# Seven products instead of eight for four of sixteen row tiles of the FFN input projection

## The chip, the cores and the metric

The kernel runs on one core of a Trainium2 chip. The metric is the device time of one execution in microseconds (us), as the median of several. One more execution was profiled; the rows shown in this document come from that one.

## The reference, cut to what matters

The network is two layers over 256 tokens with 2048 channels. Each layer has a mixer (one wide input projection, three branches, an output projection) and then a gated feed-forward block (FFN). The change is in the FFN:

```python
h = rms_norm(x, g_ffn_pre)                       # (256, 2048)
a, b = jnp.split(h @ w_ffn_in, 2, axis=-1)       # w_ffn_in (2048, 11264): a and b are (256, 5632)
x = x + rms_norm((jax.nn.silu(a) * b) @ w_ffn_out, g_ffn_post)
```

All inputs are float32.

## The kernel before, in words

**Products in two pieces.** TensorE multiplies in a reduced float32 format (F32R). So each factor is kept as two pieces, hi (rounded) and lo (what rounding left), and each product is three matmuls into one accumulator: hi by hi, lo by hi, hi by lo (L670, L671, L672). The tokens are the stationary factor, 128 channels by 128 tokens; the weights move, 128 rows by 512 columns.

**Chunks, items and blocks.** The list `chunks` holds every 512-column piece of every weight matrix, in order: for the FFN the pairs (a columns j, b columns j), j from 0 to 10, cut into two parts of 6 and 5 pairs (L599), each part followed by its share of the output projection `w_ffn_out` in four column pieces, which accumulates over the parts in the tiles `og` (L557 to L563). An item is one row tile (128 rows) of one chunk; an FFN-in chunk has 16. A block is two items, loaded together by `load` (L636): one DMA of 512 KB into a `raw` tile (`fetch`, RAWBUFS of them), one cast on ScalarE (ACT) to `whi` (L646), one subtraction on VectorE (DVE) to `wlo` (L647). There are WBLOCKS = 7 buffers for `whi` and `wlo`. All weight transfers are issued from one queue, SyncE's (SP).

**Two token halves.** `multiply(h)` does one item for the 128 tokens of half h, three matmuls. The main loop (L758) lets half 0 run up to LAG = 8 items ahead of half 1 and then alternates. So a block's twelve matmuls stand in two groups of six, and its buffers come free when half 1 has used it. The first pair of each layer's FFN (a chunk that begins a stage, `paired`) takes a and b block by block in turn; the other 20 pairs of the two layers take chunk a and then chunk b.

**Evacuation.** After the 16 items of a chunk, `ev_a` (L540) makes silu(a): a Sigmoid on ACT and a multiplication on DVE; `ev_b` (L547) multiplies by b on DVE and, D_T = 7 steps later, transposes the result on TensorE (L137) and splits it into hi and lo (L130 on ACT, L131 on DVE). These tiles, `hid`, are the stationary factor of the output projection. PSUM has eight banks: two each for the accumulators of half 0 (`mm0`) and half 1 (`mm1`), two for transposes (`tp`), two for other small products (`sc`). Tiles of 4 KB per partition come from one pool of SLOTS.

The order of instructions on each engine, and which buffer of a tag a tile takes, is laid down at build time by the framework, which starts from the order in which the code emits them; only the first block of the program (L753) is kept in the written order.

Of the kernel before, what the change touches and what calls it, by code (L numbers as in the profile page):

```python
# [11 lines left out]
F32 = mybir.dt.float32  # L12
# [3 lines left out]
ALU = mybir.AluOpType  # L16
# [17 lines left out]


LOAD = 2
RAWBUFS = 4
LAG = 8
WBLOCKS = 7
SLOTS = 22  # L40


BUDGET = 0.35
# [29 lines left out]
def trunk(ctx: ExitStack, tc: tile.TileContext, x, x_cols, positions, g_mix_post, g_ffn_post, w_in, pool_w,  # L73
# [14 lines left out]
    def nm(s):  # L88
        uid[0] += 1
        return f"{s}_{uid[0]}"  # L90
# [4 lines left out]
    def t2(tag, bufs, shape=(P, NB), dtype=F32):  # L95
        return tmp.tile(list(shape), dtype, name=nm(tag), tag=tag, bufs=bufs)
# [2 lines left out]
        return sm.tile([P, n], dtype, name=nm(tag), tag=tag, bufs=bufs)  # L99

    def ps_tp():
        return psum.tile([P, 4, P], F32, name=nm("tp"), tag="tp", bufs=2)

    def ps_sc():
        return psum.tile([P, 4, P], F32, name=nm("sc"), tag="sc", bufs=2)

    ident = cpool.tile([P, P], F32, name="ident")
    make_identity(nc, ident)
# [15 lines left out]
    def split(src, gain=None):  # L124
        t = slot([P, 2, 4, P], F32R)
        if gain is not None:
            u = t2("ta", 3, (P, 4, P))
            dve.tensor_tensor(u, src, gain.unsqueeze(2).to_broadcast([P, 4, P]), op=ALU.mult)  # L128
            src = u
        act.copy(t[:, 0], src)  # L130
        dve.tensor_tensor(t[:, 1], src, t[:, 0].bitcast(F32), op=ALU.subtract)  # L131
        return t

    def transpose4(src):
        tp = ps_tp()
        for j in range(4):
            pe.transpose(tp[:, j, :], src[:, j * P:(j + 1) * P], ident)  # L137
        return tp
# [9 lines left out]
    def defer(steps, fn, *args):  # L148
        later.append((clock[0] + steps, fn, args))
# [5 lines left out]
        for _, fn, args in due:  # L155
            fn(*args)

    def pre_norm_quad(h, c, gain):
        st["xT", h].append(split(transpose4(xs[h][:, c, :]), gain[:, 4 * c:4 * c + 4]))

    def pre_norm_rstd(h, ssq):
        tot = small("ssq_t", 1)
# [27 lines left out]
            st["ms_o", h] = small("ms_o", 1)  # L190
            gp.tensor_scalar(st["ms_o", h], tot, 1.0 / D, NORM_EPS, op0=ALU.mult, op1=ALU.add)  # L191

    def post_norm(h, gain):
        r = st["rpost", h]
        ogs = [st["og", h, c] for c in range(4)]

        def residual(c):
            xc = xs[h][:, c, :]
            dve.scalar_tensor_tensor(xc, ogs[c], r, xc, op0=ALU.mult, op1=ALU.add)  # L199
            if gain is None:  # L200
                nc.sync.dma_start(out[0, h * P:(h + 1) * P, c * NB:(c + 1) * NB], xc)

        if gain is None:
            for c in range(4):
                residual(c)
            return
        st["xT", h] = []
        residual(0)
        for c in range(4):
            defer(N_FIRST + N_STEP * c, pre_norm_quad, h, c, gain)  # L210
            if c < 3:
                defer(N_FIRST + N_STEP * c, residual, c + 1)
        defer(N_FIRST + N_STEP * 4, sum_squares, h)
# [317 lines left out]
    def ev_out(l, c):  # L531
        def f(h, ps):
            bc = gain_tile(c, h, g_mix_post[l])
            og_tile(c, h)
            post_collect(h, c, ps, bc)
            if c == 3:
                post_norm(h, par[l][:, C_GFFN:C_GFFN + 16])
        return f

    def ev_a(h, ps):  # L540
        s = t2("tb", 2)
        act.activation(s, ps, ACT.Sigmoid, scale=st["rstd", h])  # L542
        t = t2("sg", 3)
        dve.scalar_tensor_tensor(t, ps, st["rstd", h], s, op0=ALU.mult, op1=ALU.mult)  # L544
        st["sg", h] = t

    def ev_b(first):  # L547
        def f(h, ps):
            if first:
                st["hid", h] = []  # L550
            t = t2("ta", 3)
            dve.scalar_tensor_tensor(t, ps, st["rstd", h], st["sg", h], op0=ALU.mult, op1=ALU.mult)  # L552
            hid = st["hid", h]
            defer(D_T, lambda: hid.append(split(transpose4(t))))
        return f

    def ev_ffn(l, c, part, last):  # L557
        def f(h, ps):
# [20 lines left out]
    for l in range(DEPTH):  # L579
        wi = w_in[l]  # L580
        add(wi, 0, 16, Q_POOL, "xT", ev_pool(l))
        for qd in range(2):
            add(wi, 0, 16, Q_V + qd * NB, "xT", ev_v(qd))
        for qd in range(2):
            add(wi, 0, 16, Q_Q + qd * NB, "xT", ev_rot("qT", qd))
        for qd in range(2):
            add(wi, 0, 16, Q_K + qd * NB, "xT", ev_rot("kT", qd))
        for qd in range(2):
            add(wi, 0, 16, Q_R + qd * NB, "xT", ev_swish(l, qd))
        add(wi, 0, 16, Q_CG, "xT", ev_conv_g)  # L590
        add(wi, 0, 16, Q_CA, "xT", ev_conv_a(l))
        for b, c in [(b, c) for c in range(4) for b in (0, 2)] + [(1, c) for c in range(4)]:
            add(wi, 0, 16, Q_GATE + b * D + c * NB, "xT", ev_gate)
            w, name = ((w_pool_proj, "pool"), (w_conv_proj, "conv"), (w_ret_proj, "ret"))[b]
            add(w[l], 0, 8 if b == 2 else 4, c * NB, ("brT", b), ev_y(b, c), (name,))
        for c in range(4):
            add(w_out[l], 0, 16, c * NB, "mT", ev_out(l, c))
        ends.append(len(chunks))
        parts = ((0, 6), (6, 11))  # L599
        for p, (b0, b1) in enumerate(parts):  # L600
            for j in range(b0, b1):
                add(w_ffn_in[l], 0, 16, j * NB, "xT", ev_a)
                add(w_ffn_in[l], 0, 16, HIDDEN + j * NB, "xT", ev_b(j == b0))
            for c in range(4):
                add(w_ffn_out[l], b0 * 4, (b1 - b0) * 4, c * NB, "hid", ev_ffn(l, c, p, p == len(parts) - 1))
        ends.append(len(chunks))

    paired = {0} | {e for e in ends[:-1]}  # L610
    items = []
    n = 0
    while n < len(chunks):
        side = (n, n + 1) if n in paired else (n,)
        for k in range(0, chunks[n][2], LOAD):
            for m in side:
                items += [(m, k + kk) for kk in range(LOAD)]
        n += len(side)
    raws = {}
    wt = {}  # L620
    banks = {}
    loaded = [0]
    done = [0, 0]

    def fetch(i):
        n, k = items[i]
        w, r0, kt, c0 = chunks[n][:4]
        r = (r0 + k) * P
        raw = wpool.tile([P, LOAD, NB], F32, name=nm("raw"), tag="raw", bufs=RAWBUFS)
        step = LOAD if i else 1  # L630
        for kk in range(0, LOAD, step):
            nc.sync.dma_start(raw[:, kk:kk + step], w[r + kk * P:r + (kk + step) * P, c0:c0 + NB]
                              .rearrange("(k p) n -> p k n", p=P))
        raws[i] = raw

    def load():  # L636

        i = loaded[0]
        if i not in raws:
            fetch(i)  # L640
        raw = raws.pop(i)
        hi = wpool.tile([P, LOAD, NB], F32R, name=nm("whi"), tag="whi", bufs=WBLOCKS)
        lo = wpool.tile([P, LOAD, NB], F32R, name=nm("wlo"), tag="wlo", bufs=WBLOCKS)
        step = LOAD if i else 1
        for kk in range(0, LOAD, step):
            act.copy(hi[:, kk:kk + step], raw[:, kk:kk + step])  # L646
            dve.tensor_tensor(lo[:, kk:kk + step], raw[:, kk:kk + step], hi[:, kk:kk + step].bitcast(F32),  # L647
                              op=ALU.subtract)
        for kk in range(LOAD):
            wt[i + kk] = (hi[:, kk, :], lo[:, kk, :])  # L650
        loaded[0] += LOAD
# [3 lines left out]
    def load_ahead():  # L655
        while loaded[0] < min(len(items), done[1] // LOAD * LOAD + ahead[0]):
            load()

    def multiply(h):
        i = done[h]  # L660
        n, k = items[i]
        w, r0, kt, c0, lhs, evac, needs = chunks[n]
        if k == 0:
            finish({(s, q) for s in needs for q in (0, h)})
            banks[h, n] = psum.tile([P, NB], F32, name=nm("mm"), tag=f"mm{h}", bufs=2)
        ps = banks[h, n]
        a = (st[lhs + (h,)] if isinstance(lhs, tuple) else st[lhs, h])[k // 4]
        hi, lo = wt[i]
        ah, al = a[:, 0, k % 4, :], a[:, 1, k % 4, :]
        pe.matmul(ps, ah, hi, start=(k == 0), stop=False)  # L670
        pe.matmul(ps, al, hi, start=False, stop=False)  # L671
        pe.matmul(ps, ah, lo, start=False, stop=(k == kt - 1))  # L672
        if k == kt - 1:
            evac(h, ps)
        if h == 1:
            del wt[i]
        done[h] += 1
        load_ahead()
        tick()


    def begin():
# [71 lines left out]
        begin()  # L754
    ahead[0] = LOAD * WBLOCKS
    defer(16, add_job, ("trig", 0), rotary_tables(), True)
    count = [sum(chunks[n][2] for n in range(e)) for e in ends]
    for end in count:  # L758
        while done[1] < end:
            if done[0] < end:  # L760
                multiply(0)
            if done[0] == end or done[0] - done[1] > LAG:
                multiply(1)
                run_jobs(BUDGET)


def _tables():
# [52 lines left out]
```

## Time and profile before

| | us |
|---|---|
| median of 3 runs (2900.63 to 2902.14) | 2900.93 |
| the profiled execution | 2900.57 |
| span of that execution, first to last instruction | 2898.8 |

A row of the profile names a line of the kernel, an engine, what is written and read, the count, the busy time and the mean length of one instruction. PE is TensorE's matmuls and transposes, PEld its weight loads, which run beside them. A matmul's length there is the time it is in the pipeline; successive matmuls overlap, so their pitch is read from start times. Idle time is put down to whatever ended it.

### The profile page before, as it was taken

The numbers are of one execution on the slowest core, as the hardware profiler recorded it, in microseconds if no ns is written. First come the engines' busy times: TensorE is split into PE (matmuls) and PEld (weight loads), VectorE is DVE, ScalarE is ACT, GpSimd is POOL, SyncE is SP. The second block draws the span as 40 slices with busy tenths as digits, with TensorE's granted clock in tenths as the row PEclk, the third lists the DMA queues.
The fourth block names the chain that finished last, engine by engine and source line by source line (L and its number), as shares of the span: only waits on it lengthen the run. The fifth ranks groups of instructions, "written<-read, shape, count | busy, mean of one in ns | idle before, by whom it ended". The sixth has DMA issues, their size and how long they took to land.

```text
span 2898.8 us, 34028 instructions
## 1 busy us (share of the span) xinstructions
PE 2882.3 (99%) x13052; PEld 2384.2 (82%) x13052; DVE 1703.5 (59%) x1955; ACT 1283.8 (44%) x1462; POOL 83.0 (3%) x102
## 2 busy tenths in 40 slices
PE   9999999999999999999999999999999999999998
PEld 7888888888888888888888888888888888888887
DVE  6766965556555544555565579555565555445555
ACT  5443445445444444444454444454454444444443
POOL 0000000100000000000000000000000000000000
PEclk9999999999999999999999999999999999999999
DMA  8665666656666556665666656666556665566654
GB/s 293 187 184 181 189 197 189 188 190 204 183 188 193 189 192 195 189 189 193 200 189 182 186 176 186 199 189 189 191 187 197 188 190 190 194 191 191 188 196 149
DMA packets 289860, 555.07 MB, mean 191 GB/s; under 512 B 17824, under 2 KB 21152, under 8 KB 289696
## 3 DMA queue, kind: packets, MB, share of 16 engines
q1 hardware_dynamic: 289696, 552.89, 62.2%
q8 instruction: 102, 1.67, 0.2%
q14 instruction: 62, 0.51, 0.0%
HBM read 550.72 MB, written 2.10 MB: 191 GB/s over the span
## 4 chain that ended last, share of the span: by engine, by line
PE 97%; DVE 1%; DMA 1%; ACT 1%; issue 0%; POOL 0%; SPq 0%; DVEq 0%; POOLq 0%; ACTq 0%
PE mm L672 31%; PE mm L671 31%; PE mm L670 31%; PE tp L137 2%; DMA raw<-in_w_in 1%; DVE wlo L647 1%; ACT whi L646 0%; DVE x L199 0%; PE sc L402 0%; PE tp L394 0%; PE sc L358 0%; DVE ta L128 0%; DMA dt<-in_bands 0%; DMA gp<-in_g_mix_post 0%; ACT junk L142 0%
## 5 line engine op out<-in xcount | busy, mean ns | idle before, releaser
L647 DVE TENSOR_TENSOR wlo<-raw,whi 128x1024 fp32r<-128x1024 f32 (+1 forms) x1025 | 1273.5, 1243 | 1072.4 <-ACT whi L646 1056.3
L646 ACT CAST whi<-raw 128x1024 fp32r<-128x1024 f32 (+1 forms) x1025 | 1077.9, 1053 | 1427.4 <-PE mm L671 1374.7
L670 PE MATMUL mm<-whi,slot 128*128 128x512 f32 x4096 | 1605.0, 392 | 0.7 <-ACT whi L646 0.7
L672 PE MATMUL mm<-wlo,slot 128*128 128x512 f32 x4096 | 1596.2, 390 | 1.1 <-DVE wlo L647 1.1
L671 PE MATMUL mm<-whi,slot 128*128 128x512 f32 x4096 | 1595.7, 390 | 0.7 <-DVE slot L131 0.6
L672 PEld LDWEIGHTS mm<-wlo,slot 128*128 128x128 f32 x4096 | 768.8, 188 | 163.2 <-DVE wlo L647 3.6
L671 PEld LDWEIGHTS mm<-whi,slot 128*128 128x128 f32 x4096 | 769.5, 188 | 158.0 <-DVE slot L131 2.1
L670 PEld LDWEIGHTS mm<-whi,slot 128*128 128x128 f32 x4096 | 769.2, 188 | 156.4 <-ACT whi L646 1.7
L315 DVE SCALAR_TENSOR_TENSOR slot<-slot,par,slot 128x229 f32<-128x229 f32 (+23 forms) x240 | 102.1, 481 | 0.3
L511 POOL TENSOR_TENSOR slot<-slot,tb 128x512 f32<-128x512 f32 x32 | 43.3, 1352 | 639.2 <-DVE tb L510 592.2
L130 ACT CAST slot<-tp 128x512 fp32r<-128x512 f32 x60 | 35.2, 586 | 30.1 <-PE tp L137 30.1
L131 DVE TENSOR_TENSOR slot<-tp,slot 128x512 fp32r<-128x512 f32 x60 | 41.2, 687 | 7.3 <-ACT slot L130 7.3
L191 POOL TENSOR_SCALAR ms_o<-ssq_t 128x1 f32<-128x1 f32 x8 | 1.5, 190 | 1518.1 <-DVE ssq_t L189 1518.1
L498 ACT ACTIVATE sg<-mm,rstd 128x512 f32<-128x512 f32 x48 | 33.0, 688 | 24.4 <-PE mm L672 24.1
L542 ACT ACTIVATE tb<-mm,rstd 128x512 f32<-128x512 f32 x44 | 30.2, 686 | 26.8 <-PE mm L672 26.8
L544 DVE SCALAR_TENSOR_TENSOR sg<-mm,rstd,tb 128x512 f32<-128x512 f32 x44 | 32.9, 748 | 15.0 <-ACT tb L542 15.0
L137 PEld LDWEIGHTS tp<-ident,ta 128*128 128x128 f32 x272 | 34.0, 141 | 8.4
L137 PE MATMUL tp<-ident,ta 128*128 128x128 f32 x272 | 40.6, 271 | 0.0
L552 DVE SCALAR_TENSOR_TENSOR ta<-mm,rstd,sg 128x512 f32<-128x512 f32 x44 | 33.0, 751 | 12.9 <-PE mm L672 12.7
L130 ACT CAST slot<-ta 128x512 fp32r<-128x512 f32 x40 | 24.8, 620 | 18.6 <-DVE ta L128 18.5
L131 DVE TENSOR_TENSOR slot<-ta,slot 128x512 fp32r<-128x512 f32 x40 | 27.4, 686 | 1.5 <-ACT slot L130 1.4
L510 DVE TENSOR_TENSOR tb<-mm,sg 128x512 f32<-128x512 f32 x32 | 22.1, 691 | 9.1 <-PE mm L672 8.8
(109 smaller groups left out, 507.2 us busy)
## 6 DMA issues: line engine op xcount, KB each, us to landing
raw<-in_w_in SPq DMA_DIRECT2D x367, 512.0 KB, 3.7
raw<-in_w_ffn_in SPq DMA_DIRECT2D x352, 512.0 KB, 3.8
raw<-in_w_ffn_out SPq DMA_DIRECT2D x176, 512.0 KB, 3.6
raw<-in_w_out SPq DMA_DIRECT2D x64, 512.0 KB, 3.7
raw<-in_w_ret_proj SPq DMA_DIRECT2D x32, 512.0 KB, 3.7
raw<-in_w_pool_proj SPq DMA_DIRECT2D x16, 512.0 KB, 3.6
raw<-in_w_conv_proj SPq DMA_DIRECT2D x16, 512.0 KB, 3.9
dt<-in_decays SPq DMA_DIRECT2D x12, 256.0 KB, 3.8
```

The costliest lines, as they stand in the source:

```text
L130: act.copy(t[:, 0], src)
L131: dve.tensor_tensor(t[:, 1], src, t[:, 0].bitcast(F32), op=ALU.subtract)
L137: pe.transpose(tp[:, j, :], src[:, j * P:(j + 1) * P], ident)
L315: dve.scalar_tensor_tensor(acc[:, ct, s:], hT[:, ct, :SEQ - s], w[:, TAPS - 1 - s:TAPS - s], acc[:, ct, s:], op0=ALU.mult, op1=ALU.add)
L498: act.activation(s, ps, ACT.Sigmoid, scale=st["rstd", h])
L511: gp.tensor_tensor(m, m, t, op=ALU.add)
L552: dve.scalar_tensor_tensor(t, ps, st["rstd", h], st["sg", h], op0=ALU.mult, op1=ALU.mult)
L646: act.copy(hi[:, kk:kk + step], raw[:, kk:kk + step])
L647: dve.tensor_tensor(lo[:, kk:kk + step], raw[:, kk:kk + step], hi[:, kk:kk + step].bitcast(F32), op=ALU.subtract)
L670: pe.matmul(ps, ah, hi, start=(k == 0), stop=False)
L671: pe.matmul(ps, al, hi, start=False, stop=False)
L672: pe.matmul(ps, ah, lo, start=False, stop=(k == kt - 1))
```

## The change

Let the last four row tiles (k = 12 to 15) of a pair of column chunks be a 2x2 block problem: the rows are the two token halves, the inner dimension is tiles 12, 13 and tiles 14, 15, the columns are chunk a and chunk b. Before, this takes eight block products of two items each. After, it takes seven, with sums and differences of weight blocks (T1 to T4, on DVE, in place in the `raw` tiles, then split into hi and lo like any block), of token blocks (S1 to S4, `token_sums`, once per layer) and of the results (on DVE, in `mixed_product` and `ev_b`). It is done for the 20 pairs in `fast`; the first pair of each layer stays as it was. Row tiles 0 to 11 stay as they were. The order of blocks in such a pair is, with n for chunk a, m for chunk b and the first row tile behind it: n0 n2 n4 n6 n8 b11 t1 n10 b21 b22 m0 t2 m2 t3 m4 t4 m6 m8 m10. The seven products b11, t1, b21, b22, t2, t3, t4 are done once, in half 0's course; half 1 steps over them.

Beside that: silu(a) becomes one Silu on ACT; the FFN is cut into four parts (3, 3, 3 and 2 pairs) instead of two; `raw` has 6 buffers instead of 4; SLOTS is 20 instead of 22; transposes and small products share four PSUM banks, and b11, t1, t2, t3 use them too.

```diff
-RAWBUFS = 4
+RAWBUFS = 6
-SLOTS = 22
+SLOTS = 20
...
-        return psum.tile([P, 4, P], F32, name=nm("tp"), tag="tp", bufs=2)
+        return psum.tile([P, 4, P], F32, name=nm("tp"), tag="sc", bufs=4)
...
+    def token_sums():
+        u = st["u"]
+        a11, a12, a21, a22 = (u[:, h, 2 * i:2 * i + 2] for h in range(2) for i in range(2))
+        s = slot([P, 4, 2, P])
+        dve.tensor_tensor(s[:, 0], a21, a22, op=ALU.add)
+        dve.tensor_tensor(s[:, 1], s[:, 0], a11, op=ALU.subtract)
+        dve.tensor_tensor(s[:, 2], a11, a21, op=ALU.subtract)
+        dve.tensor_tensor(s[:, 3], a12, s[:, 1], op=ALU.subtract)
+        hi, lo = slot([P, 4, 2, P], F32R), slot([P, 4, 2, P], F32R)
+        act.copy(hi, s)
+        dve.tensor_tensor(lo, s, hi.bitcast(F32), op=ALU.subtract)
+        st["S"] = (hi, lo)
...
     def ev_a(h, ps):
-        s = t2("tb", 2)
-        act.activation(s, ps, ACT.Sigmoid, scale=st["rstd", h])
         t = t2("sg", 3)
-        dve.scalar_tensor_tensor(t, ps, st["rstd", h], s, op0=ALU.mult, op1=ALU.mult)
+        act.activation(t, ps, ACT.Silu, scale=st["rstd", h])
...
             t = t2("ta", 3)
+            if mixed:
+                dve.tensor_tensor(t, st["sum", h], ps, op=ALU.add)
+                ps = t
             dve.scalar_tensor_tensor(t, ps, st["rstd", h], st["sg", h], op0=ALU.mult, op1=ALU.mult)
...
+    def ev_a_sum(h, t, y):
+        u = t2("ta", 3)
+        dve.tensor_tensor(u, t, y, op=ALU.add)
+        ev_a(h, u)
...
-        parts = ((0, 6), (6, 11))
+        parts = ((0, 3), (3, 6), (6, 9), (9, 11))
...
+    fast = {n for n, ch in enumerate(chunks) if ch[5] is ev_a and n not in paired}
...
     def load():
...
+        if kind == "t1":
+            kept["b12"] = fetch(i, n + 1, k)
+            dve.tensor_tensor(kept["b11"], kept["b12"], kept["b11"], op=ALU.subtract)
+            raw = kept["b11"]
+        elif kind == "t2":
+            raw = kept["b22"]
+        elif kind == "t3":
+            raw = kept["b12"]
+        elif kind == "t4":
+            dve.tensor_tensor(kept["b21"], kept["b21"], kept["b22"], op=ALU.subtract)
+            raw = kept["b21"]
...
             act.copy(hi[:, kk:kk + step], raw[:, kk:kk + step])
             dve.tensor_tensor(lo[:, kk:kk + step], raw[:, kk:kk + step], hi[:, kk:kk + step].bitcast(F32),
                               op=ALU.subtract)
+        if kind == "b22":
+            dve.tensor_tensor(kept["b12"], raw, kept["b12"], op=ALU.subtract)
+            dve.tensor_tensor(raw, raw, kept["b11"], op=ALU.subtract)
...
+    def mixed_product(kind, n, k, w):
...
+        if kind == "b11":
+            x = bank(x_part(0))
+            if last:
+                st["sum", 1] = t2("dt", 2)
+                act.copy(st["sum", 1], x)
+        elif kind == "b21":
+            y = product((0, n), "mm0", x_part(0), w, last)
+            if last:
+                ev_a_sum(0, st["sum", 1], y)
+        elif kind == "t1":
+            bank(s_part(0))
+        elif kind == "b22":
+            product((0, n + 1), "mm0", s_part(3), w, False)
+        elif kind == "t4":
+            y = product((1, n), "mm1", x_part(1), w, last)
+            if last:
+                s = st["sum", 1]
+                ev_a_sum(1, s, y)
+                dve.tensor_tensor(s, s, banks["t1", n], op=ALU.add)
+        elif kind == "t2":
+            x = bank(s_part(1))
+            if last:
+                s = st["sum", 1]
+                dve.tensor_tensor(s, s, x, op=ALU.add)
+                st["sum", 0] = t2("dt", 2)
+                dve.tensor_tensor(st["sum", 0], s, banks["t1", n], op=ALU.add)
+        elif kind == "t3":
+            x = bank(s_part(2))
+            if last:
+                s = st["sum", 1]
+                dve.tensor_tensor(s, s, x, op=ALU.add)
```

In this listing `product` does the three matmuls of one item into the named bank, `x_part(h)` is the token block of half h, and `s_part(i)` one of the four token sums.

## Rows read from the trace of the kernel before

**Rows 1.** The page's busy times and shares of the span.

```profile
PE 2882.3 (99%) x13052; PEld 2384.2 (82%) x13052; DVE 1703.5 (59%) x1955; ACT 1283.8 (44%) x1462; POOL 83.0 (3%) x102
```

**Rows 2.** The chain that ended last, by engine.

```profile
PE 97%; DVE 1%; DMA 1%; ACT 1%; issue 0%; POOL 0%; SPq 0%; DVEq 0%; POOLq 0%; ACTq 0%
```

**Rows 3.** Windows of an FFN-in pair and FFN-out: length; PE, PEld, DVE, ACT, POOL; clock, DMA.

```profile
912.14:956.61 44.47, 44.47 (x201) 36.84 (x200) 23.77 (x23) 19.20 (x20) 0.00 (x0) 1.00 0.65 190
1000.90:1110.00 109.10, 109.10 (x483) 90.38 (x482) 49.23 (x41) 45.19 (x47) 0.00 (x0) 1.00 0.59 194
```

**Rows 4.** Waits in layer 0's FFN (662 to 1436 us): total, times, longest.

```profile
ACT whi L646 <- PE mm L671: 391.8, 255, 1.7
DVE wlo L647 <- ACT whi L646: 336.9, 260, 1.5
...
PEld mm L671 <- DVE slot L131: 0.3, 1, 0.3
```

**Rows 5.** Timeline of PE, first and last of 89 successive matmuls in an FFN-in chunk.

```profile
906.49 0.39 PE L670 MATMUL mm<-whi,slot 128*128 128x512 f32 x1
...
926.45 0.39 PE L671 MATMUL mm<-whi,slot 128*128 128x512 f32 x1
```

**Rows 6.** Groups of instructions in the window of one FFN-in pair (912.14 to 956.61).

```profile
L647 DVE TENSOR_TENSOR wlo<-raw,whi 128x1024 fp32r<-128x1024 f32 x17 | 20.8, 1225 | 20.5 <-ACT whi L646 20.4
L646 ACT CAST whi<-raw 128x1024 fp32r<-128x1024 f32 x16 | 16.9, 1054 | 22.8 <-PE mm L671 22.8
L670 PEld LDWEIGHTS mm<-whi,slot 128*128 128x128 f32 x64 | 12.0, 188 | 2.4
...
L552 DVE SCALAR_TENSOR_TENSOR ta<-mm,rstd,sg 128x512 f32<-128x512 f32 x2 | 1.5, 751 | 0.6 <-PE mm L672 0.6
L544 DVE SCALAR_TENSOR_TENSOR sg<-mm,rstd,tb 128x512 f32<-128x512 f32 x2 | 1.5, 748 | 0.7 <-ACT tb L542 0.7
L131 DVE TENSOR_TENSOR slot<-tp,slot 128x512 fp32r<-128x512 f32 x2 | 1.4, 688 | 0.3 <-ACT slot L130 0.3
L542 ACT ACTIVATE tb<-mm,rstd 128x512 f32<-128x512 f32 x2 | 1.4, 686 | 1.2 <-PE mm L672 1.2
L130 ACT CAST slot<-tp 128x512 fp32r<-128x512 f32 x2 | 1.2, 588 | 1.3 <-PE tp L137 1.3
```

**Rows 7.** Groups over the whole run, shapes kept apart.

```profile
L563 DVE TENSOR_TENSOR slot<-slot,mm 128x512 f32<-128x512 f32 x16 | 11.0, 686 | 9.3 <-PE mm L672 9.3
L472 DVE TENSOR_TENSOR tb<-mm,tr 128x256 f32<-128x256 f32 x16 | 6.6, 415 | 0.0
L560 ACT COPY slot<-mm 128x512 f32<-128x512 f32 x16 | 9.3, 583 | 9.7 <-PE mm L672 9.7
L491 ACT ACT_TABLE_LOAD x1 | 1.3, 1283 | 0.0
```

**Rows 8.** Timeline of one block's cast and subtraction in FFN-in.

```profile
915.32 1.05 ACT L646 CAST whi<-raw 128x1024 fp32r<-128x1024 f32 x1 [1.55 <-PE mm L671]
916.41 1.23 DVE L647 TENSOR_TENSOR wlo<-raw,whi 128x1024 fp32r<-128x1024 f32 x1 [1.38 <-ACT whi L646]
```

**Rows 9.** DMA issues of the FFN-in weights: count, KB each, us to landing.

```profile
raw<-in_w_ffn_in SPq DMA_DIRECT2D x352, 512.0 KB, 3.8
```

**Rows 10.** Timeline at the end of a part: half 0's `ev_b` and the making of `hid`.

```profile
978.37 0.75 DVE L552 SCALAR_TENSOR_TENSOR ta<-mm,rstd,sg 128x512 f32<-128x512 f32 x1
...
982.25 0.60 PE L137 MATMUL tp<-ident,ta 128*128 128x128 f32 x4
...
982.89 0.59 ACT L130 CAST slot<-tp 128x512 fp32r<-128x512 f32 x1 [0.29 <-PE tp L137]
983.77 0.68 DVE L131 TENSOR_TENSOR slot<-tp,slot 128x512 fp32r<-128x512 f32 x1
```

More of the change, by code (lines that the diff above doesn't have):

```diff
@@ L101, in ps_tp @@
     def ps_tp():
-        return psum.tile([P, 4, P], F32, name=nm("tp"), tag="tp", bufs=2)
+        return psum.tile([P, 4, P], F32, name=nm("tp"), tag="sc", bufs=4)
     def ps_sc():
-        return psum.tile([P, 4, P], F32, name=nm("sc"), tag="sc", bufs=2)
+        return psum.tile([P, 4, P], F32, name=nm("sc"), tag="sc", bufs=4)
     ident = cpool.tile([P, P], F32, name="ident")
@@ L156, in tick, with pre_norm_quad @@
             fn(*args)
-    def pre_norm_quad(h, c, gain):
-        st["xT", h].append(split(transpose4(xs[h][:, c, :]), gain[:, 4 * c:4 * c + 4]))
+    def pre_norm_quad(h, c, gain, mixed):
+        tp, g = transpose4(xs[h][:, c, :]), gain[:, 4 * c:4 * c + 4]
+        if not (mixed and c == 3):
+            st["xT", h].append(split(tp, g))
+            return
+        if h == 0:
+            st["u"] = slot([P, 2, 4, P])
+        u = st["u"][:, h]
+        dve.tensor_tensor(u, tp, g.unsqueeze(2).to_broadcast([P, 4, P]), op=ALU.mult)
+        st["xT", h].append(split(u))
+        if h == 1:
+            defer(6, token_sums)
+    def token_sums():
[10 more added lines that the diff above has]
+        st["S"] = (hi, lo)
     def pre_norm_rstd(h, ssq):
@@ L191, in post_collect, with post_norm @@
             gp.tensor_scalar(st["ms_o", h], tot, 1.0 / D, NORM_EPS, op0=ALU.mult, op1=ALU.add)
-    def post_norm(h, gain):
+    def post_norm(h, gain, mixed=False):
         r = st["rpost", h]
@@ L209, in post_norm @@
         for c in range(4):
-            defer(N_FIRST + N_STEP * c, pre_norm_quad, h, c, gain)
+            defer(N_FIRST + N_STEP * c, pre_norm_quad, h, c, gain, mixed)
             if c < 3:
@@ L536, in f @@
             if c == 3:
-                post_norm(h, par[l][:, C_GFFN:C_GFFN + 16])
+                post_norm(h, par[l][:, C_GFFN:C_GFFN + 16], True)
         return f
     def ev_a(h, ps):
-        s = t2("tb", 2)
-        act.activation(s, ps, ACT.Sigmoid, scale=st["rstd", h])
         t = t2("sg", 3)
-        dve.scalar_tensor_tensor(t, ps, st["rstd", h], s, op0=ALU.mult, op1=ALU.mult)
+        act.activation(t, ps, ACT.Silu, scale=st["rstd", h])
         st["sg", h] = t
     def ev_b(first):
-        def f(h, ps):
+        def f(h, ps, mixed=False):
             if first:
@@ L610, in trunk, with plan @@
     paired = {0} | {e for e in ends[:-1]}
+    fast = {n for n, ch in enumerate(chunks) if ch[5] is ev_a and n not in paired}
     items = []
+    count = {}
+    def plan(kind, n, k):
+        items.extend((kind, n, k + kk) for kk in range(LOAD))
     n = 0
     while n < len(chunks):
[L614 to L618, printed above, removed]
+        if n in fast:
+            for k in (0, 2, 4, 6, 8):
+                plan("", n, k)
+            plan("b11", n, 12)
+            plan("t1", n, 12)
+            plan("", n, 10)
+            plan("b21", n, 14)
+            plan("b22", n, 14)
+            plan("", n + 1, 0)
+            plan("t2", n, 12)
+            plan("", n + 1, 2)
+            plan("t3", n, 12)
+            plan("", n + 1, 4)
+            plan("t4", n, 14)
+            for k in (6, 8, 10):
+                plan("", n + 1, k)
+            n += 2
+        else:
+            side = (n, n + 1) if n in paired else (n,)
+            for k in range(0, chunks[n][2], LOAD):
+                for m in side:
+                    plan("", m, k)
+            n += len(side)
+        count[n] = len(items)
     raws = {}
@@ L623, in trunk, with fetch @@
     done = [0, 0]
-    def fetch(i):
-        n, k = items[i]
+    def fetch(i, n=None, k=None):
+        if n is None:
+            n, k = items[i][1:]
         w, r0, kt, c0 = chunks[n][:4]
@@ L634, in fetch @@
         raws[i] = raw
+        return raw
+    kept = {}
     def load():
         i = loaded[0]
-        if i not in raws:
-            fetch(i)
-        raw = raws.pop(i)
+        kind, n, k = items[i]
+        if kind == "t1":
[10 more added lines that the diff above has]
+        elif kind == "b22":
+            raw = kept[kind] = fetch(i, n + 1, k)
+        else:
+            if i not in raws:
+                fetch(i)
+            raw = raws.pop(i)
+            kept[kind] = raw
         hi = wpool.tile([P, LOAD, NB], F32R, name=nm("whi"), tag="whi", bufs=WBLOCKS)
@@ L657, in load_ahead, with product, x_part, s_part @@
             load()
+    def product(key, tag, a, w, stop):
+        first = key not in banks
+        if first:
+            banks[key] = psum.tile([P, NB], F32, name=nm("mm"), tag=tag, bufs=4 if tag == "sc" else 2)
+        ps = banks[key]
+        pe.matmul(ps, a[0], w[0], start=first, stop=False)
+        pe.matmul(ps, a[1], w[0], start=False, stop=False)
+        pe.matmul(ps, a[0], w[1], start=False, stop=stop)
+        return ps
+    def mixed_product(kind, n, k, w):
+        kk, last = k % 2, k % 2 == 1
+        def x_part(h):
+            a = st["xT", h][k // 4]
+            return a[:, 0, k % 4, :], a[:, 1, k % 4, :]
+        def s_part(i):
+            return st["S"][0][:, i, kk, :], st["S"][1][:, i, kk, :]
+        def bank(a):
+            return product((kind, n), "sc", a, w, last)
+        if kind == "b11":
[9 more added lines that the diff above has]
+            bank(s_part(0))
+        elif kind == "b22":
+            product((0, n + 1), "mm0", s_part(3), w, False)
+        elif kind == "t4":
+            y = product((1, n), "mm1", x_part(1), w, last)
+            if last:
+                assert items[done[1]][1:] > (n, 11)
+                s = st["sum", 1]
[13 more added lines that the diff above has]
+                dve.tensor_tensor(s, s, x, op=ALU.add)
@@ L659, in multiply @@
     def multiply(h):
         i = done[h]
[L661 to L676, printed above, removed]
-        done[h] += 1
+        kind, n, k = items[i]
+        done[h] += 1
+        if kind:
+            if h == 0:
+                mixed_product(kind, n, k, wt.pop(i))
+        else:
+            w, r0, kt, c0, lhs, evac, needs = chunks[n]
+            if k == 0:
+                finish({(s, q) for s in needs for q in (0, h)})
+            mixed = n in fast or n - 1 in fast
+            last = k == (11 if mixed else kt - 1)
+            a = (st[lhs + (h,)] if isinstance(lhs, tuple) else st[lhs, h])[k // 4]
+            ps = product((h, n), f"mm{h}", (a[:, 0, k % 4, :], a[:, 1, k % 4, :]), wt[i], last and n not in fast)
+            if h == 1:
+                del wt[i]
+            if last and n not in fast:
+                evac(h, ps, *([True] if mixed else []))
@@ L678, in multiply @@
         load_ahead()
-        tick()
+        if h == 0 or not kind:
+            tick()
     def begin():
@@ L756, in trunk @@
     defer(16, add_job, ("trig", 0), rotary_tables(), True)
-    count = [sum(chunks[n][2] for n in range(e)) for e in ends]
-    for end in count:
+    for end in [count[e] for e in ends]:
         while done[1] < end:
@@ L764, in trunk @@
                 run_jobs(BUDGET)
+                while done[1] < min(done[0], end) and items[done[1]][0]:
+                    multiply(1)
 def _tables():
```

## The prediction

> **What bounds the kernel now.** I read the page's busy shares first. PE is busy for 2882.3 of the 2898.8 us of the span, DVE for 59%, ACT for 44% [rows 1]. Busy matmuls overlap, so the share alone proves little; the chain that ended last settles it: 97% of it is PE [rows 2]. Next the windows, since the change touches one stage only. One FFN-in pair, from one `ev_a` of half 0 to the next, takes 44.47 us; PE works throughout at a granted clock of 1.00, DVE for 23.77 us (53%), ACT for 19.20 us (43%), the DMA engines for 65% [rows 3]. The waits of that stage tell the same: ACT's cast waits for PE to give a weight buffer back (391.8 us in all), DVE waits for that cast (336.9 us), and PE's one wait on the two is 0.3 us [rows 4]. So matmuls taken out of FFN-in shorten the kernel for as long as DVE and ACT keep ahead, and DVE is where the change puts its additional work.
>
> **What is removed on PE.** The block problem of a pair took 8 products of 2 items and 3 matmuls, 48; it takes 42 after. That is 6 matmuls in each of 20 pairs, 120 in all. Their pitch, from 906.49 to 926.45 over 88 steps, is 0.2268 us [rows 5]. 120 x 0.2268 = 27.2 us. The four parts change no number of matmuls or transposes.
>
> By the Trainium skill (TensorE: Matmul & The Clock Gate, Back-to-back issue gap) a warm matmul of 512 columns takes about 216 ns from start to start; the trace's pitch is 5% longer, and by the page's figure the 120 would give back 25.9 us, 1.3 us less. The sum here goes by the row.
>
> **What DVE gets, per pair.** Before: 16 subtractions, two each of L544, L552 and L131, near the 23.77 us of the window. After:
> - 19 blocks are split instead of 16 (seven products, twelve plain blocks): 19 x 1.225 = 23.3 us [rows 6].
> - T1 to T4 are four 128x1024 subtractions. The trace has none with float32 output; the row nearest in shape, L647, gives 1.225 us [rows 6], 4.9 us. Bounds: 128x512 takes 686 ns [rows 7], so two of those, 1.37 us, is the upper end, and one of them the lower.
> - Eight sums of 128x512 (one after b21, two after t2, one after t3, two after t4, one in each `ev_b`), with one operand in PSUM, as L563: 8 x 0.686 = 5.5 us [rows 7].
> - L552 and L131 stay, 1.5 and 1.4 us; L544 goes [rows 6].
>
> Together 36.6 us, against a PE time of 44.47 - 6 x 0.2268 = 43.1 us: 85%. DVE still fits, on average.
>
> **What it looks like inside the pair.** The dense part is from b11 to t4. As half 1 steps over the products, PE does 16 groups of six matmuls between the start of b11 and the start of t4: ten of half 0 (b11, t1, n10, b21, b22, m0, t2, m2, t3, m4) and six of half 1. A group is 6 x 0.2268 = 1.36 us, so 21.8 us. In that time DVE must do ten splits, four T, four sums and one L131: 14 x 1.225 + 4 x 0.686 + 0.69 = 20.6 us, 94%. The remaining 21.3 us of the pair hold only 16.0 us of DVE work. So the dense part is the place to watch, and its cushion is the lead with which blocks are ready. A buffer comes free four groups before half 0's first use of it (7 blocks, less the lag of 4 and the block in work), 5.4 us; the lo piece is read two matmuls later, 5.9 us. From the start of the cast to the end of the subtraction are 916.41 + 1.23 - 915.32 = 2.3 us [rows 8]. So the lead is 3.6 us. In the dense part buffers even come back sooner than that, since a product's buffers are free after half 0 alone. I take no stall there: 20.6 us of work fits into 21.8, with 3.6 us in hand for the order of the work. The bounds: nothing, or the second rival's price.
>
> **ACT.** Per pair 19 casts at 1.054, two Silu at about 0.69 (as the Sigmoid), one copy at 0.58, two L130: 23.2 us of 43.1 [rows 6, 7], hidden behind PE. Going from Sigmoid to Silu and back at each change of stage adds perhaps three table loads of 1.28 us [rows 7], under the 3.6 us lead; uncovered they would cost 4 us once.
>
> **Transfers.** The bytes are the same. But four of the six `raw` tiles are held by b11/T1, b12/T3, b21 and b22/T2 for most of the dense part. A transfer must start 3.8 us (landing, [rows 9]) + 1.05 us (cast) ahead of the block's first matmul. T1's tile comes free when T2 is made, that is in the load of b22, and the plain tiles of n10, m0 and m2 come back right after their splits; if any free tile is taken, m4, m6 and m8 find one in time. Cost nothing; otherwise the third rival.
>
> **Four parts.** The boundaries are new work for `hid`: a part's output projection needs the last pair's `hid` at its item 8 (three pairs) or already at item 4 (the last part, two pairs) of half 0, where before it was item 20 or 16. From `ev_b` of half 0 to a finished `hid` takes 983.77 + 0.68 - 978.37 = 6.1 us [rows 10], to its hi piece 5.1 us; the additional sum comes before the transposes, which wait for their step anyway. Item 8 comes eight groups of six after half 0's last matmul, 10.9 us: covered. Item 4 comes four groups and a transpose (0.60 us at most) later, 6.0 us, with lo due 0.2 us behind; with 0.3 us from PE's last matmul to `ev_b`, hi is ready in 5.4 and lo in 6.4 us. Rather than 0.1 I put in 0.7 us for each layer, since DVE has splits to do in between, in all 1.4 us; bounds 0 and the whole chain, 12 us. The 32 additional accumulations into `og` (4 columns, 2 halves, 2 more parts, 2 layers, 0.686 us, [rows 7]) fall in FFN-out, where DVE works 49.23 of 109.10 us [rows 3]; `token_sums` (four of at most 0.42 us, a cast, a split, [rows 6, 7]) has a whole pair of time. Both nothing; without that cover 22 us and some 8 us.
>
> **The sum.** Against the profiled execution's 2900.57 us: 2900.57 - 27.2 + 1.4 = 2874.8; the median of the runs stands 0.36 us above it, 2875.1. For small waits at the stage changes I add 1 us: 2876.
>
> **Rivals.**
> 1. DVE is late now and then, 0.2 to 1 us a pair, and 4 to 20 us of the gain go: 2880 to 2896. For it: 94% in the dense part, with four T and four sums that hang on results made just before. Against it: the 3.6 us lead and 5 us of DVE slack in the rest of each pair.
> 2. DVE's queue stands still, and the kernel gets slower. Each T must be cast (1.05 us) before DVE can split it, and sums wait for PE (L552 waited 0.64 us where it came first). If nothing else fills these, 4 x 1.05 + 4 x 0.64 = 6.8 us come to the dense part's 20.6: 27.4 against 21.8, 5.6 late, less the lead of 3.6 leaves 2.0 us of PE standing per pair, 40 us: 2915. It decides from 27.2 / 20 = 1.36 us a pair on. Against it: other splits are ready to fill in, if the build-time order puts them there.
>    The Trainium skill (Perfetto Trace Analysis, Identifying the Most-Contended Engine) judges DVE by its busy share but TensorE by that of its weight loads: after the change about 36.84 - 6 x 0.188 = 35.7 of 43.1 us, 83%, just below DVE's 85%, which by that rule makes DVE the engine to relieve. In the trace of before (PEld 36.84, DVE 23.77 of 44.47 us, [rows 3]) the rule and the chain name the same engine, PE.
> 3. The `raw` tiles are taken strictly in turn. Then m4's transfer waits for t3's split and m8's for t4's. Their matmuls are due 14 and 19 groups after the start of b11, at 19.0 and 25.8 us, so these splits would have to end by 14.2 and 21.0 us (4.85 us for landing and cast). If DVE does them a block (1.2 us) and more behind that, each comes some 1.5 us late: 3 us a pair, 60 us, 2935. For it: nothing in the trace excludes it, since with four `raw` tiles of equal lifetimes turn and freedom look alike. Against it: a pool that hands out whichever tile is free has m4's transfer under way from T2 on, 4 splits earlier.
> 4. The change gives back what it brings: half 0 and half 1 wait at all eight part boundaries for about 1.5 us each, 24 us: 2899. Against it: the 10.9 us worked out above.
>
> **How the numbers follow.** About 0.2% (6 us) is what a measurement of this kernel can tell from no change. Forecast (2872 to 2880): 0.62. Rival 1: 0.15. Rival 2: 0.08. Rival 3: 0.07. Rival 4: 0.08, no change. Faster 0.77, the same 0.08, slower 0.15. The range 2871 to 2898 holds the forecast, rival 1 and part of 4, about 0.8; the two slower rivals are left out.
>
> **What would show it.** Right: an FFN-in pair of 43.1 us with PE without a wait, DVE at some 36 to 37 us in it, 12168 matmuls in all. Wrong: waits of PE for `wlo` or `whi` in the dense part (rival 1 or 2, DVE busy or idle there), casts waiting for the transfer of `raw` (rival 3), PE waiting for L131 at the part boundaries (rival 4).

## The result, and the profile after

The changed kernel takes 2876.61 us (median of 4 runs, 2874.08 to 2877.45) against 2901.17 us before (4 runs, 2900.63 to 2902.14): the ratio is 0.9914 (95% interval 0.9896 to 0.9931), 24.6 us less. The whole interval lies below 1. The forecast was 2876, the range 2871 to 2898. The profiled execution took 2875.82 us with a span of 2874.1 us.

The page's busy times and the chain by engine, which answer to [rows 1] and [rows 2]:

```profile
PE 2855.9 (99%) x12932; PEld 2362.9 (82%) x12932; DVE 1947.7 (68%) x2253; ACT 1356.4 (47%) x1547; POOL 83.1 (3%) x102
...
PE 98%; DVE 1%; DMA 0%; POOL 0%; ACT 0%; issue 0%; SPq 0%; DVEq 0%; POOLq 0%; ACTq 0%
```

PE has exactly 120 instructions less than before, 12932 for 13052, DVE 298 more, and PE is still what the end hangs on. The window of one pair done by seven products, from one Silu of half 0 to the next (length, PE, PEld, DVE, ACT, POOL, clock, DMA share, GB/s), answers to [rows 3]:

```profile
936.66:979.75 43.09, 43.09 (x195) 35.71 (x194) 34.75 (x36) 22.50 (x26) 0.00 (x0) 1.00 0.59 196
```

The pair is 1.38 us shorter, 43.09 for 44.47; six matmuls at the old pitch are 1.36. PE works throughout. DVE went from 23.77 to 34.75 us, ACT from 19.20 to 22.50. The groups in that window, against [rows 6] (kind, count, busy time in us and mean in ns, idle time before and what ended it; an instruction cut by an end of the window counts as one, so 20 splits stand for 19):

```profile
L726 DVE TENSOR_TENSOR wlo<-raw,whi 128x1024 fp32r<-128x1024 f32 x20 | 24.0, 1219 | 4.3 <-ACT whi L725 4.2
L725 ACT CAST whi<-raw 128x1024 fp32r<-128x1024 f32 x20 | 20.8, 1053 | 16.1 <-PE mm L748 12.2 <-DVE raw L705 2.6 <-DVE raw L730 1.3
...
L730 DVE TENSOR_TENSOR raw<-raw,raw 128x1024 f32<-128x1024 f32 x1 | 1.2, 1225 | 0.0
...
L790 DVE TENSOR_TENSOR dt<-dt,mm 128x512 f32<-128x512 f32 x1 | 0.7, 689 | 0.2 <-PE mm L749 0.2
```

The operations of which the trace of before had no row cost what their nearest rows said: making T2 (L730) 1.225 us, a sum with an operand in PSUM (L790) 0.69 us. ACT does wait for T1 (L705, 2.6 us) and T2 (L730, 1.3 us), as the second rival has it, but the wait goes no further than ACT; PE shows none.

PE's waits behind the first 100 us, the whole list (total, times, longest):

```profile
PE tp L140 <- DVE x L226: 1.6, 4, 0.6
PE mm L747 <- ACT slot L133: 0.2, 1, 0.2
```

L140 and L226 are the changes of stage (the residual before the transposes of a norm); L133 is the making of `hid`, at a part boundary.

**Where the 24.7 us of span went.** Two marks cut the program: the first and the last product with the mixer's output gain, and the last residual. Before (kind, count, shortest, median and longest ns, first and last start):

```profile
L186 DVE TENSOR_TENSOR slot<-mm,gp x16: 683/688/692, 643.5 to 2162.0; 128x512 f32<-128x512 f32 x16
L199 DVE SCALAR_TENSOR_TENSOR x<-slot,rpost,x x32: 741/745/752, 709.9 to 2894.1; 128x512 f32<-128x512 f32 x32
```

After:

```profile
L213 DVE TENSOR_TENSOR slot<-mm,gp x16: 678/686/692, 645.3 to 2151.0; 128x512 f32<-128x512 f32 x16
L226 DVE SCALAR_TENSOR_TENSOR x<-slot,rpost,x x32: 736/744/753, 711.7 to 2869.8; 128x512 f32<-128x512 f32 x32
```

Up to the first mark is the first layer's mixer, which the change hardly touches: 1.8 us later. Between the two marks of the first line lie the first FFN and the second mixer: 1518.5 us before, 1505.7 after, -12.8. From there to the last residual lies the second FFN: 732.1 and 718.8, -13.3. The tail is 0.4 us shorter. These two stretches, called A and B below, are read in every run; ten pairs of 1.36 us would be 13.6 in each. "Start" is the first mark.

### The profile page after: what moved, and what is told of

Read it like the earlier page. It is cut to its first block, busy times and chain, and to the rows that moved or that the text cites. A ratio compares the mean times of both kernels' runs of the same rounds, so it can differ in the third digit from the quotient of the medians.

```text
span 2874.1 us, 34293 instructions
## 1 busy us (share of the span) xinstructions
PE 2855.9 (99%) x12932; PEld 2362.9 (82%) x12932; DVE 1947.7 (68%) x2253; ACT 1356.4 (47%) x1547; POOL 83.1 (3%) x102
## 4 chain that ended last, share of the span: by engine, by line
PE 98%; DVE 1%; DMA 0%; POOL 0%; ACT 0%; issue 0%; SPq 0%; DVEq 0%; POOLq 0%; ACTq 0%
PE mm L748 32%; PE mm L749 32%; PE mm L747 32%; PE tp L140 2%; DVE x L226 0%; PE sc L429 0%; PE tp L421 0%; PE sc L385 0%; DVE wlo L726 0%; DVE ta L131 0%; DMA dt<-in_bands 0%; DMA par<-in_params 0%; POOL rpost_a L210 0%; PE sc L411 0%; PE tp L406 0%
## 5 line engine op out<-in xcount | busy, mean ns | idle before, releaser
L726 DVE TENSOR_TENSOR wlo<-raw,whi 128x1024 fp32r<-128x1024 f32 (+1 forms) x1085 | 1336.9, 1240 | 738.0 <-ACT whi L725 725.6
L725 ACT CAST whi<-raw 128x1024 fp32r<-128x1024 f32 (+1 forms) x1085 | 1135.4, 1052 | 1283.5 <-PE mm L748 1148.2
L133 ACT CAST slot<-tp 128x512 fp32r<-128x512 f32 x60 | 35.2, 586 | 83.3 <-PE tp L140 83.3
L578 DVE TENSOR_TENSOR ta<-dt,mm 128x512 f32<-128x512 f32 x40 | 27.4, 684 | 29.9 <-PE mm L749 29.9
L597 DVE TENSOR_TENSOR slot<-slot,mm 128x512 f32<-128x512 f32 x48 | 32.8, 684 | 13.0 <-PE mm L749 13.0
L140 PEld LDWEIGHTS tp<-ident,ta 128*128 128x128 f32 x272 | 34.0, 141 | 8.4
L140 PE MATMUL tp<-ident,ta 128*128 128x128 f32 x272 | 40.6, 271 | 0.0
L569 ACT ACTIVATE sg<-ta,rstd 128x512 f32<-128x512 f32 x40 | 29.0, 725 | 10.5 <-DVE ta L588 10.5
L580 DVE SCALAR_TENSOR_TENSOR ta<-ta,rstd,sg 128x512 f32<-128x512 f32 x40 | 30.0, 749 | 1.0
L133 ACT CAST slot<-ta 128x512 fp32r<-128x512 f32 x36 | 22.4, 621 | 16.4 <-DVE ta L131 16.2
```

Source lines behind the costliest of these rows:

```text
L597: dve.tensor_tensor(o, o, ps, op=ALU.add)
```

## The experiments

My theory: the time follows PE, so each pair gives back its six matmuls; DVE's additional work costs nothing as long as it fits into the pair; the other edits are nearly free. Against it stand the rivals: DVE late or standing still, transfers late for want of `raw` tiles, the gain lost at the part boundaries. Each ratio is to the kernel before, run beside it on the same chip; its medians there lie between 2900.7 and 2902.9 us.

| run | median us | start | A | B |
|---|---|---|---|---|
| before | 2901.2 | 643.5 | 1518.5 | 732.1 |
| changed | 2876.6 | 645.3 | 1505.7 | 718.8 |
| rest_only | 2904.9 | 647.6 | 1519.2 | 732.3 |
| layer0_only | 2889.2 | 645.0 | 1505.6 | 732.3 |
| six_fewer | 2873.3 | 643.2 | 1505.0 | 718.5 |
| sigmoid | 2874.2 | 649.1 | 1505.6 | 718.8 |
| raw5 | 2875.2 | 644.6 | 1505.7 | 718.7 |
| raw4 | 2963.0 | 643.4 | 1552.8 | 759.8 |
| dve4 | 2874.0 | 643.0 | 1505.7 | 718.7 |
| dve8 | 2876.1 | 645.2 | 1506.7 | 719.3 |
| dve12 | 2944.1 | 646.2 | 1540.1 | 752.5 |
| parts5 | 2877.0 | 647.0 | 1505.8 | 719.0 |
| raw5_dt3 | 2872.7 | 641.1 | 1505.6 | 718.9 |

The three columns on the right are from one profiled execution each. Start wanders by some 6 us (643.0 to 649.1) between kernels that have the same start in the code; A and B repeat within 0.2 us where nothing in the FFN differs. So small effects are read from A and B.

### The other edits without the products

```diff
-    fast = {n for n, ch in enumerate(chunks) if ch[5] is ev_a and n not in paired}
+    fast = set()
```

> The changed kernel with no pair done by seven products: four parts, one Silu, six raw tiles, 20 slots and the shared PSUM banks stay. If only the removed matmuls count: the time of the kernel before, 2900 to 2903 us, with 0 to 1.4 us for the part boundaries. If the other edits carry part of the gain (less DVE work for silu, more transfers ahead): 2890 to 2897 us.

Measured 2904.92 us, ratio 1.0012 (1.0003 to 1.0022): slower than before, by more than I allowed. A and B hold 0.7 and 0.2 us of it; the rest, some 2.8 us, lies in the start. So Silu, the parts, the tiles and the banks, taken together, carry no part of the gain. Against this run the products give 13.5 us in A and 13.5 in B, 27.0 for 120 matmuls.

### Half of the pairs

```diff
+    fast = {n for n in fast if n < ends[1]}
```

> Seven products in the ten pairs of the first layer only. If each pair gives back its six matmuls (1.36 us) and no more: half of the gain, 2888 to 2890 us. If DVE falls behind over several pairs (a backlog that grows), the first layer alone gives more than half: under 2887 us is then not possible, but the FFN of the first layer shows pairs longer than 43.1 us.

2889.19 us, ratio 0.9957 (0.9943 to 0.9972). A is that of the changed kernel (1505.6), B that of the run before this one (732.3). Half of the pairs give half of the gain. Nor does a backlog grow within a layer: in the changed kernel the pairs from 785.13, 936.66 and 979.75 us take 43.12, 43.09 and 43.10 us.

### The matmuls alone

```diff
-        pe.matmul(ps, ah, hi, start=(k == 0), stop=False)
...
+        ffn_in = evac is ev_a and n not in paired
+        if not (ffn_in and k in (13, 14) and h == 1):
+            pe.matmul(ps, ah, hi, start=(k == 0), stop=False)
...
```

> The kernel before with six matmuls left out in each of the same 20 pairs (row tiles 13 and 14 of chunk a for half 1, so that part of the sum is missing), nothing else changed. This is the price of the matmuls alone. If a removed matmul is worth its pitch of 0.2268 us: 2901.2 - 27.2 = 2874 us. By the 216 ns of the Trainium skill's page (TensorE: Matmul & The Clock Gate, Back-to-back issue gap) 2875.3 us. If the changed kernel hides losses in its pairs it stands above this run by their size; I expect 1 to 3 us.

2873.31 us, ratio 0.9904 (0.9889 to 0.9919). A and B are 13.5 and 13.6 us shorter, 27.1 / 120 = 0.226 us a matmul, the pitch of [rows 5]. The 216 ns of the Trainium skill (TensorE: Matmul & The Clock Gate, Back-to-back issue gap) would make 25.9 us; that section gives them for an isolated matmul and about 131 ns for a sustained stream, which would make 15.7. The runs bear out neither. The changed kernel is 0.7 and 0.3 us longer in A and B, and that is all it loses in the FFN.

### Silu as before

```diff
+        s = t2("tb", 2)
+        act.activation(s, ps, ACT.Sigmoid, scale=st["rstd", h])
         t = t2("sg", 3)
-        act.activation(t, ps, ACT.Silu, scale=st["rstd", h])
+        dve.scalar_tensor_tensor(t, ps, st["rstd", h], s, op0=ALU.mult, op1=ALU.mult)
```

> The changed kernel with silu made as before, a Sigmoid on ACT and a multiplication on DVE: two more DVE instructions of 0.75 us in each pair, 34.8 + 1.5 = 36.3 of 43.1 us. If DVE has room: no change, 2875 to 2878 us. If DVE in the dense part is at its limit: up to 1.5 us a pair, 2880 to 2907 us.

2874.22 us, ratio 0.9910 (0.9895 to 0.9925), A and B as in the changed kernel. Saving the two multiplications is worth nothing here, since DVE has room for them. The profiled execution is the slowest of the four (2879.53 us); its late start, 649.1 us, is taken up below.

### Fewer raw tiles

```diff
-RAWBUFS = 6
+RAWBUFS = 5
```

and the same with 4.

> The changed kernel with five raw tiles instead of six. If a transfer takes any free tile: m0 gets the tile of n10, m2 that of T1, each in time; no change, 2875 to 2879 us. If tiles are used strictly in turn: m0 waits for T2 and later ones for t3 and t4, over 2 us a pair, 2915 us and more.

> The changed kernel with four raw tiles, all held by b11, b12, b21 and b22. By either theory m0's transfer can start only when T2 is made, some 3 to 4 us too late for its matmuls: PE waits, 3 to 6 us a pair, 2935 to 3000 us, with casts that wait for the transfer. If this makes no difference, I have the lead of the loads wrong.

Five make no difference (2875.18 us, A and B unchanged), as expected if transfers take any free tile; by strict turns it would have been 2915 us and more, so the third rival falls. Four cost 86 us: A is 47.1 us longer, 4.7 a pair, B 41.0. What waits, in one pair of the run with four (965 to 1015 us):

```profile
ACT whi L725 <- DMA raw<-in_w_ffn_in: 17.0, 9, 5.2
DVE wlo L726 <- ACT whi L725: 8.3, 6, 3.1
...
PEld mm L747 <- ACT whi L725: 4.3, 3, 2.7
```

Here the chain that the third rival described is seen: a cast stands 5.2 us for its transfer, DVE behind it for the cast, PE's weight loads behind both. So a late transfer does cost PE its time as that rival said, but for want of a free tile, with four of them, and not because tiles are taken in turn.

### More work for DVE

```diff
+        for _ in range(2 if kind in ("t1", "t2", "t3", "t4") else 0):
+            spare = t2("junk", 1, (P, LOAD, NB), mybir.dt.bfloat16)
+            dve.tensor_tensor(spare, raw, hi.bitcast(F32), op=ALU.subtract)
```

with 1, 2 and 3 in place of the 2: four, eight and twelve more instructions a pair.

> The changed kernel with four more 128x1024 subtractions per pair on DVE, one behind the split of each of t1 to t4, into a tile that nobody reads: 34.8 + 4.7 = 39.5 of 43.1 us. If DVE is limited by its sum over the pair: no change, 2875 to 2879 us. If the dense part (then 25 us of work against 21.8 us, with a lead of 3.6 us) is what counts: 0 to 0.5 us a pair, up to 2887 us; if the order of the queue is already at its limit: 4.7 us a pair, 2970 us.

> The same with eight more subtractions per pair, two at each place: 34.8 + 9.3 = 44.1 us of DVE work against 43.1 of PE. By the sum over the pair: 1 us a pair more, 2896 us. By the dense part (30 us of work against 21.8, lead 3.6): 4 to 5 us a pair, 2960 to 2980 us.

> The changed kernel with twelve more subtractions per pair on DVE that nobody reads, three at each of t1 to t4. Eight cost at most 0.1 us a pair in the trace; back to back an instruction takes about 1.14 us, so the pair's DVE work is now about 35 + 13.7 = 48.5 us against 43.1 of PE. If DVE's sum over the pair is the limit: some 3 to 5 us a pair, less the lead of 3.6 us and what the output projection makes up at each of the eight parts: 2920 to 2960 us. If it is the order in the queue that matters and not the sum: no clear loss here either, below 2885 us.

Four cost nothing (2874.00 us), eight at most 1.0 us in A and 0.5 in B (2876.14 us), twelve 34.4 and 33.7 us (2944.12 us). Eight were to cost some 20 us by the sum and at least 84 by the dense part; both expectations miss. Twelve came out in the range forecast by the sum, 2920 to 2960 us. By the windows of a pair, two successive ones of the run with eight and one of the run with twelve:

```profile
937.11:979.84 42.73, 42.73 (x193) 35.13 (x192) 40.97 (x43) 20.31 (x23) 0.00 (x0) 1.00 0.58 185
979.84:1023.07 43.23, 43.23 (x196) 35.69 (x196) 42.87 (x44) 22.31 (x25) 0.00 (x0) 1.00 0.62 195
```

```profile
965.77:1012.81 47.04, 45.19 (x195) 36.68 (x194) 47.04 (x48) 22.29 (x25) 0.00 (x0) 0.96 0.55 179
```

With twelve, DVE is busy for all 47.04 us and the pair is as long as DVE's work: now DVE sets the time. With eight it is busy for 40.97 of 42.73 and 42.87 of 43.23 us, nearly all the time, and PE stands in neither window. So the sum over the pair is the limit, just above eight, and the dense part is not. That blocks loaded ahead carry PE over the dense part is my reading; their lead was not measured. I had the sum too high, since I added up lengths. In a row without waits DVE's instructions overlap; three splits of the changed kernel, 1.22 us each, took 3.49 us (start, length, kind, count):

```profile
936.54 3.49 DVE L726 TENSOR_TENSOR wlo<-raw,whi 128x1024 fp32r<-128x1024 f32 x3
```

This also bears on the busy-share rule of the Trainium skill (Perfetto Trace Analysis, Identifying the Most-Contended Engine): in the run with eight, DVE is busy for 96% of the pair and PEld for 82%, so by the rule DVE is the engine to relieve; the pair is nevertheless as long as PE's matmuls. Here DVE's share named the engine only when it reached the whole, as with twelve.

### More part boundaries

```diff
-        parts = ((0, 3), (3, 6), (6, 9), (9, 11))
+        parts = ((0, 3), (3, 5), (5, 7), (7, 9), (9, 11))
```

> The changed kernel with five parts of 3, 2, 2, 2 and 2 pairs instead of four. If only a part of two pairs makes PE wait for the hid tiles, at its item 4 and for at most 0.7 us: four such parts a layer instead of one, the FFN of a layer 1 to 2 us longer, 2878 to 2880 us in all. If every boundary costs 1.5 us (the rival that takes the whole gain): one more a layer, 3 us, and each boundary shows waits of that size.

2876.97 us; A and B are 0.1 and 0.2 us longer. Even four parts of two pairs a layer cost next to nothing, less than I expected, and the fourth rival falls. PE's list for the first FFN has one wait of 0.2 us for `hid`, as in the changed kernel.

### A version that goes further

```diff
-RAWBUFS = 6
+RAWBUFS = 5
...
-            b = t2("dt", 2, (P, 4, P))
+            b = t2("dt", 3, (P, 4, P))
```

and 3 for 2 at the other uses of `dt`.

> The changed kernel with five raw tiles and a third dt tile, so that the third band table of the first layer's pooling needn't wait for the first one's release. In all kernels with five or six raw tiles PE stood 2.0 to 3.7 us for that transfer, in the kernel before 1.4 us. If the wait is for the tile: it goes, 2 to 3 us less than the changed kernel, 2872 to 2874 us. If it is for the crowded transfers of the start: the wait stays, 2875 us.

2872.74 us (median of 4 runs, 2871.65 to 2873.77), ratio to before 0.9903 (0.9887 to 0.9920). The wait for the band table is gone and the start is the earliest of all runs, 641.1. Its first 110 us have these waits of PE:

```profile
PE sc L858 <- DVE slot L826: 1.5, 1, 1.5
PE mm L747 <- ACT whi L725: 1.1, 1, 1.1
PE mm L749 <- DVE wlo L726: 0.8, 2, 0.4
```

The changed kernel has these in its first 100:

```profile
PE sc L385 <- DMA dt<-in_bands: 3.0, 1, 3.0
PE mm L747 <- ACT whi L725: 1.7, 1, 1.7
...
```

The intervals of this version and of the changed kernel overlap; so a gain in the median over the changed kernel is not shown. What is shown is that the wait for the band table was for the tile: with five `raw` tiles and two `dt` tiles it is still 2.7 us, with the third it is gone.

## Why the prediction was right

- **The removed matmuls**: 27.2 us forecast, 27.1 with the matmuls alone, 27.0 as the difference between the changed kernel and the one without the products. Count (3 x 4056 = 12168 matmuls on the weights) and pitch hold.
- **DVE per pair**: 36.6 us forecast, 34.75 measured. The terms were right one by one; adding up lengths overstated DVE's time here by some 5%, since its instructions overlap where they follow each other without a wait.
- **The dense part and the lead**: no stall taken, none found. My account of it as the place to watch was wrong, though: by it (21.8 us and a lead of 3.6) eight more instructions should have cost 4 to 5 us a pair, and they cost at most 0.1. Rivals 1 and 2 fall: PE shows no wait for `whi` or `wlo` behind the start, and DVE decides only from somewhere between 8 and 12 more instructions a pair.
- **ACT**: 23.2 us forecast, 22.50 measured; three more table loads a run (six for three), with no wait of PE for ACT behind the start beyond the 0.2 us for `hid`.
- **Transfers**: nothing forecast, nothing found with six or five tiles.
- **Part boundaries**: 1.4 us forecast. The kernel without products is 0.7 and 0.2 us longer than before in A and B, 0.9 in all, which holds this and everything else in the FFN. Rival 4 falls.
- **Small waits at the stage changes**: 1 us forecast, a margin that no row gave, and for the wrong place. The stage changes show 1.6 us of PE waiting for L226, against 1.4 for the same wait in the run with six matmuls fewer, whose other code is that of before. The loss lies in the start: 1.8 us up to the first mark in the profiled execution, about 1.6 between the medians (24.6 gained of 27.2 - 1.0). So the main term and its path, PE without a wait, are shown. That the total came out within 1 us is partly luck: the boundaries were 0.5 us too dear and the start was missing.

What makes the start longer is settled in part. PE's wait for the band table was 1.4, 1.4 and 1.0 us in the three kernels with four `raw` tiles, 2.7 with five, and 2.0 to 3.7 with six; a third `dt` tile removes it. For the 1.7 us between before and changed the traces show two parts (the matmuls that waited, in the kernel before and in the changed one):

```profile
78.00 1.83 PE L358 MATMUL sc<-dt,slot 128*128 128x128 f32 x14 [1.35 <-DMA dt<-in_bands]
78.68 1.83 PE L385 MATMUL sc<-dt,slot 128*128 128x128 f32 x14 [3.03 <-DMA dt<-in_bands]
```

These matmuls start 0.7 us later, since the transfer was issued 0.3 us later and took 4.84 us for 4.48. The other 1.0 us is order: between the two groups of band matmuls PE has 18 weight matmuls before and 13 in the changed kernel, so it comes to the second group sooner and stands longer. Why the order and the transfer differ stays open.

The spread of the start from run to run is in part the clock. PE's waits up to 110 us add up to 4.7 us before, 6.2 in the changed kernel and 6.3 in the run with Sigmoid. In that run, whose start is the latest, the granted clock was 0.83 from 10 to 20 us and 0.50, its lower level throughout, from 80 to 85 us, behind the wait for the band table. How waits and clock add up to each start is not worked out.

## What to carry to other kernels

Where one engine works without a gap and the next has idle time, work can be traded from the first to the second at the price that the pitch of the first gives, and in this kernel the second's room was its idle time over a whole pair, not in the densest stretch. The room can be measured by adding work that nobody reads until the time moves. Before a stage that keeps tiles longer is called free, the number of tiles should be lowered by one and by two: here five were enough and four cost 86 us.

## What the runs showed of the hardware

After PE had stood 1.7 us for its first weights, the granted clock fell in the changed kernel's profiled execution: 0.88 in the window from 10 to 20 us, where before, with a wait of 0.7 us, it was 1.00; and the starts of successive matmuls stood 0.43 us apart instead of 0.227, the lower of the clock's two levels, 1.2 GHz:

```profile
9.07 0.63 PE L747 MATMUL mm<-whi,slot 128*128 128x512 f32 x1
9.49 0.63 PE L748 MATMUL mm<-whi,slot 128*128 128x512 f32 x1
...
12.45 0.40 PE L749 MATMUL mm<-wlo,slot 128*128 128x512 f32 x1
12.69 0.40 PE L747 MATMUL mm<-whi,slot 128*128 128x512 f32 x1
```

From 9.07 to 12.45 us eight matmuls took 3.4 us instead of 1.8. So in this execution a short wait at the start was paid for twice. That is not so each time: in the run without the products PE stood 1.6 and 0.7 us for its first weights, and the clock stayed at 1.00 from 10 to 20 us. Behind the wait for the band table it stayed at 1.00 in the changed kernel (3.0 us) and was 0.71 from 80 to 85 us in the run without the products (3.7 us). Where PE waits for DVE now and then, it falls in some pairs: in the run with twelve more DVE instructions it was 0.96 over the pair shown, in which PE stood 1.9 us at a stretch, and 1.00 from 944.19 to 990.39 us, where the longest wait was 0.8 us.
